# Moving the last GpSimd subtractions of the branch stage to VectorE in a three-term fp32 decoder layer

## The chip, the cores and the metric

One core of a Trainium2 chip runs the whole kernel in one launch. The metric is the device time in microseconds (us) of that core, as the median of several executions. The engines are named as in the profile: PE is TensorE (PEld its weight loads), DVE is VectorE, ACT is ScalarE, POOL is GpSimd, SP is SyncE, which here issues nearly all DMAs.

## The reference

One layer of a decoder trunk on 1024 tokens of width 1024, in float32:

```
u = rmsnorm(x) @ w_in            # 12 blocks of columns: q,k,v; retention q,k,v,g; lru x,y; 3 gates
od  = diff_attention(...)        # branch 0
o_r = silu(rg) * group_norm(retention(...))   # branch 1
o_l = rg_lru(...) * gelu(ly)     # branch 2
g   = sigmoid(gates)
merged = g0*(od @ w_branch[0]) + g1*(o_r @ w_branch[1]) + g2*(o_l @ w_branch[2])
x = x + merged @ w_out
x = x + cross_attention(rmsnorm(x), rmsnorm(mem))
x = x + relu(rmsnorm(x) @ w1)**2 @ w2
out = rmsnorm(x)
```

The part that matters here is `merged` (three products of 1024x1024 by 1024x1024, each gated and summed) and the first use of `w_out` behind it.

## The kernel before, in words

Every product is taken in a split format. A float32 matrix is held as a high part (`hi`, a rounded copy that ACT makes) and a low part (`lo`, source minus `hi`, one subtraction). The helper `split` (lines 70 and 71) issues both: the copy always on ACT, the subtraction on the engine that it is given, VectorE by default. A product is three matmuls (lines 59, 60, 61): hi by hi, hi by lo, and `lo` of the left factor by `hi`. So TensorE needs the `hi` of a left factor at line 59 and its `lo` two matmuls later, at line 61.

The branch products, the projections before them and the first MLP product run by a Strassen-Winograd scheme: a pair of weight units of 128 columns is cut into blocks A11 to A22, four sums of them are made by VectorE (`left`, line 1117), and seven block products (numbered k = 1 to 7) replace eight. For each k one left factor, here called a unit (tile `wu`, 128x512), is split by `prepare` (through `pair_unit`). The units are made ahead of the products: `h_products` writes all of them into one list (`self.line`), and each product first calls `ahead`, which emits the next one of the list. A unit takes 12 matmuls.

The pairs of the three branches are the last 12 of that list (index p from m on). For k = 1 and 2, `prepare` always puts the subtraction on VectorE. For the others it takes the engine that `prep` hands it: before, that is VectorE for k = 6 and 4 and GpSimd for k = 7, 5 and 3.

`branch` runs three times, in the order 1, 0, 2 (branch number). It runs 28 products each time. VectorE sums each finished product out of PSUM (lines 1182 to 1187 for the scheme's own sums, line 828 for the final block), multiplies by the sigmoid of the gate (line 829) and adds the accumulator of the branch before (line 831). The result goes to DRAM (line 833); in the last branch the half of the rows with n >= 4 is split straight into a resident tile (`block<-y`). Meanwhile `load_blocks` and `fill_block` load the right factors of the next branch (`block<-block`, 128x1024 subtractions on VectorE). In the last branch the left half of `w_out` is also loaded, in four pieces through one buffer `wst`, and split: VectorE takes pieces 0 and 2, GpSimd pieces 1 and 3. The other half of `w_out` is split in four further pieces by `weight` (tile `w`), whose default engine is GpSimd. Then `w_out` begins (tile `pso`).

Each engine runs its own instructions in the order in which a planner put them at compile time, by its modelled times and by program order; `after` adds that the `hi` copies of units ("wsplit") and the weight loads ("wdma") keep the order of the program. At run time nothing is reordered: an instruction that waits holds up what is behind it on its engine, and a DMA that waits on SP's queue holds up the DMAs behind it.

Of the kernel before, what the change touches and what calls it, by code (L numbers as in the profile page):

```python
# [49 lines left out]
class Kernel:  # L50
# [596 lines left out]
    def h_products(self):  # L647


        nc, v, a = self.nc, self.nc.vector, self.a  # L650
# [6 lines left out]
        cs, m = [{} for _ in jobs], len(jobs)  # L657
# [6 lines left out]
        pairs = [(c, [UNITS[kind](n, i) for i in range(2)]) for (kind, n), c in zip(jobs, cs)]  # L664
# [3 lines left out]

        def prep(p, k):
            self.pair_load(p, *pairs[p])  # L670
            self.prepare(k, pairs[p][0], v if p >= m and k in (6, 4) else nc.gpsimd)

            turns = [x for x in (0, m - 2, m + 2, m + 6, m + 10) if x <= p < x + 2]
            q, at = (p + 1, 6) if not turns else (turns[0] + 2, 3 if p > 1 else 4)
            if k == at and p == (turns or [p])[0] and q < len(pairs):
                self.pair_load(q, *pairs[q])
# [3 lines left out]
        for q in range(m, m + 12, 4):  # L680
            seq += [(q + p, k) for p in range(2) for k in self.ORDER]
            seq += [(q + p, k) for k in (self.ORDER if q < m + 8 else self.LAST) for p in (2, 3)]
        self.line = collections.deque([lambda x=x: prep(*x) for x in seq])

        def run(p, k):
# [44 lines left out]
        for p in range(2):  # L730
            run(p, 1)
            yield
# [6 lines left out]
        for k in self.H_FIRST[1:]:  # L739
            for p in range(2):  # L740
                run(p, k)
        for p in range(2, m - 2):
            for k in self.ORDER:
                run(p, k)
# [67 lines left out]
    def branch(self, order, i, right, bw, sps, nxt):  # L812

        nc, v = self.nc, self.nc.vector
        after, load = (None, None) if nxt is None else self.load_blocks(nxt)
        mT = [[None, None], [None, None]]
        cs = self.bcs[order]

        def emit(n, j, x, y):
            rows, sl = slice(n * P, (n + 1) * P), slice(j * HB, (j + 1) * HB)  # L820
            sg = bw.tile([P, HB], F32, tag="sg", name="sgb", bufs=5)
            nc.sync.dma_start(sg, self.gsp[i * D + n * P:i * D + (n + 1) * P, sl])
            nc.scalar.activation(sg, sg, AF.Sigmoid)
            if order > 0:
                pv = bw.tile([P, HB], F32, tag="pv", name="pv", bufs=3)
                nc.sync.dma_start(pv, self.acc[order - 1][rows, sl])
            o = bw.tile([P, HB], F32, tag="y", name="y", bufs=4)
            v.tensor_tensor(o, x, y, op=ALU.add)
            v.tensor_tensor(o, o, sg, op=ALU.mult)
            if order > 0:  # L830
                v.tensor_tensor(o, o, pv, op=ALU.add)
            if nxt is not None or n < 4:
                nc.sync.dma_start(self.acc[order][rows, sl], o)
            else:
                self.split(mT[j][1][:, n % 4, :], o)

        def run(p, k):
            self.ahead()
            self.product(k, cs[p], right, self.p6(sps), lambda e, j, x, y: emit(2 * p + e, j, x, y))

        for p in range(2):
            for k in self.ORDER:
                run(p, k)

                if (p, k) == (0, 1):
                    next(self.loading)
                elif (p, k) == (0, 2):
                    self.fill_block()
        if nxt is not None:
            for at, k in enumerate(self.ORDER):  # L850
                run(2, k)
                if at > 0:
                    next(load)
                run(3, k)
            self.loading = load
            return after
        w, units = [], 0
        for k in self.LAST:
            run(2, k)
            run(3, k)  # L860

            if k == 1:
                mT[0][1] = self.block(self.slotA)
            elif k == 6:
                mT[1][1] = self.block(self.slotB)
            elif k in (2, 3):
                j = 3 - k
                mT[j][0] = self.block(self.slotA)
                x = self.acc[2][:, j * HB:(j + 1) * HB].rearrange("(k p) c -> p k c", p=P)
                self.fill_block(mT[j][0], x)  # L870

            if k in (7, 5, 3, 4):
                if k in (7, 3):
                    w.append(self.block(self.slotB))
                q = units % 2
                self.split(w[-1][:, 2 * q:2 * q + 2, :], wst, (v, nc.gpsimd)[q])
                units += 1
            if k in (1, 7, 5, 3):
                wst = bw.tile([P, 2, HB], F32, tag="wst", name="wst")
                self.after("hdma", nc.sync.dma_start(wst, self.a["w_o"][0, units].rearrange("p (k c) -> p k c", k=2)))  # L880
        self.fill_block()
        return mT, w
# [468 lines left out]
    def run(self):  # L1351
        tc, nc, a = self.tc, self.nc, self.a
        pool = lambda name, bufs=1, side="right", **kw: tc.tile_pool(name=name, bufs=bufs, side=side, reuse_waits="tile", **kw)
        self.setup()
        with pool("slotA", bufs=4, side="left") as self.slotA:
            self.n_gates, self.gate_order = 0, [b * 8 + n for b in (1, 0, 2) for n in range(8)]
            with pool("ret") as self.rp, pool("rps", space=PSUM) as self.rps:
                self.retention(pool)
            with pool("att") as self.ap, pool("aps", space=PSUM) as self.aps:
                self.attention()  # L1360
            with pool("slotB", bufs=4) as self.slotB:
                with pool("sps", space=PSUM) as sps:
                    with pool("sp") as self.sp:
                        self.sps = sps
                        for _ in self.hp:
                            pass
                    with pool("bw") as bw:
                        right = self.branch(0, 1, self.right, bw, sps, 0)
                        right = self.branch(1, 0, right, bw, sps, 2)
                        mT, w0 = self.branch(2, 2, right, bw, sps, None)  # L1370
                A, B = self.slotA, self.slotB
                with pool("work") as work:
                    with pool("xps", bufs=2, space=PSUM) as xps:
                        w = [[w0[u // 2][:, u % 2 * 2:u % 2 * 2 + 2, :] for u in range(4)]]
                        w.append([self.weight(a["w_o"][1, u], 2) for u in range(4)])
                        hx = [[self.block(s) for s in (B, A)]]
                        self.w_out(0, mT, w, hx[0], work, xps)
                        hx.append([self.block(s) for s in (A, B)])
                        self.w_out(1, mT, w, hx[1], work, xps)
                        self.mem_slot()  # L1380
                        self.mem_norm(work)
                        g = self.xattn(hx, work, xps)
                    with pool("mps", space=PSUM) as self.mps:
                        self.xa_last(g)
                        self.mlp_in()
                    with pool("m2ps", bufs=6, space=PSUM) as m2ps:
                        self.mlp_out(m2ps)
# [76 lines left out]
```

## Time and profile before

| | |
|---|---|
| median of 3 runs | 2423.28 us (2419.88 to 2424.56) |
| profiled execution: its own time / its span | 2424.15 us / 2422.4 us |
| mean granted TensorE clock | 0.981 |
| PE busy over the span | 2319.7 us (96%) |
| DVE busy | 1888.0 us (78%) |
| ACT busy | 1041.4 us (43%) |
| POOL busy | 955.9 us (39%) |
| branch stage, first moved unit to the start of `w_out` | about 1243 to 1521 us |

The span goes from the first to the last instruction of the program; the execution's own time is 1.75 us longer. "Busy" adds up the time in which an engine had an instruction in work; an instruction that waits for a resource inside the engine still counts as busy. In a timeline a row gives the start (us from the span's start), the duration, the engine, the line, the tiles written and read, and in brackets the idle time before it with what ended it.

### The profile page before, as it was taken

What the parts mean: (1) busy time and instruction counts of PE and PEld (TensorE: products, weight loads), DVE (VectorE), ACT (ScalarE), POOL (GpSimd) and SP (SyncE); (2) the same over time, 40 slices, a digit from 0 to 9 for tenths busy, and PEclk for the clock granted to TensorE, in tenths of its full rate; (3) what the DMA queues carried; (4) which work ended last, traced back from release to release, by engine and by line L of the source; (5) the groups of instructions that cost most, each with busy time, mean ns of one, the idle gap of its engine ahead of it and who ended that gap; (6) DMA issues with size and microseconds to landing.
All of it is one profiled execution on the core that took longest, in us unless ns stands there. A gap on an engine that the chain in (4) does not pass through costs nothing. (4 is left out here: it accounts for less than half of the span.)

```text
span 2422.4 us, 31108 instructions
## 1 busy us (share of the span) xinstructions
PE 2319.7 (96%) x11156; PEld 1913.1 (79%) x11156; DVE 1888.0 (78%) x2909; ACT 1041.4 (43%) x1817; POOL 955.9 (39%) x621
## 2 busy tenths in 40 slices
PE   9999999999999998999999988999989999899998
PEld 7888878888887876777887767778768888788886
DVE  7677487878797788798787898344788888788896
ACT  5443355555555543554354444135442222343333
POOL 1122212222215444455431223034155555598863
PEclk9999999999999999999999999999999999999999
DMA  5222122222215354543576687343225443744341
GB/s 173 81 87 70 58 70 60 64 71 70 62 49 180 127 162 162 174 134 136 178 266 240 228 287 239 105 146 119 97 83 183 152 144 135 254 167 166 121 165 70
DMA packets 135994, 335.12 MB, mean 138 GB/s; under 512 B 17040, under 2 KB 27281, under 8 KB 135840
## 3 DMA queue, kind: packets, MB, share of 16 engines
q1 hardware_dynamic: 135264, 331.30, 41.4%
q8 instruction: 89, 1.46, 0.2%
q10 hardware_dynamic: 576, 1.84, 0.2%
q14 instruction: 65, 0.53, 0.1%
HBM read 227.64 MB, written 97.05 MB: 134 GB/s over the span
## 5 line engine op out<-in xcount | busy, mean ns | idle before, releaser
L59 PE MATMUL ps<-block,wu 128*128 128x512 f32 x1428 | 568.6, 398 | 27.2 <-DVE sf L1187 10.4
L61 PE MATMUL ps<-block,wu 128*128 128x512 f32 x1428 | 565.3, 396 | 10.2 <-DVE wu L71 10.2
L60 PE MATMUL ps<-block,wu 128*128 128x512 f32 x1428 | 561.9, 394 | 0.8 <-DVE block L71 0.8
L71 POOL TENSOR_TENSOR wu<-st,wu 128x512 fp32r<-128x512 f32 x144 | 227.3, 1585 | 303.4 <-ACT wu L70 290.4
L59 PEld LDWEIGHTS ps<-block,wu 128*128 128x128 f32 x1428 | 272.4, 191 | 89.0 <-DVE sf L1187 11.3
L61 PEld LDWEIGHTS ps<-block,wu 128*128 128x128 f32 x1428 | 271.2, 190 | 75.1 <-DVE wu L71 13.3
L60 PEld LDWEIGHTS ps<-block,wu 128*128 128x128 f32 x1428 | 271.8, 190 | 61.0 <-DVE block L71 1.3
L70 ACT CAST wu<-st 128x512 fp32r<-128x512 f32 x240 | 141.9, 620 | 210.1 <-DVE st L1117 94.1
L71 POOL TENSOR_TENSOR w<-st,w 128x1024 fp32r<-128x1024 f32 x50 | 124.6, 2501 | 176.7 <-ACT w L70 176.5
L59 PE MATMUL ps<-wu,hu 128*128 128x512 f32 x456 | 179.4, 394 | 8.0 <-ACT wu L70 4.2
L60 PE MATMUL ps<-wu,hu 128*128 128x512 f32 x456 | 178.9, 392 | 0.9 <-POOL wu L71 0.8
L61 PE MATMUL ps<-wu,hu 128*128 128x512 f32 x456 | 178.6, 392 | 0.0
L71 POOL TENSOR_TENSOR wu<-sf,wu 128x512 fp32r<-128x512 f32 x63 | 122.2, 1954 | 131.9 <-ACT wu L70 95.8
L1273 DVE TENSOR_TENSOR acc<-acc,ps 128x512 f32<-128x512 f32 x184 | 118.1, 679 | 19.8 <-PE ps L61 19.4
L71 DVE TENSOR_TENSOR hu<-sth,hu 128x1024 fp32r<-128x1024 f32 x53 | 118.1, 2231 | 14.3 <-ACT hu L70 13.6
L466 ACT ACTIVATE p<-sc,mx 128x256 f32<-128x256 f32 (+7 forms) x128 | 94.8, 742 | 69.9 <-DVE mx L463 50.1
L71 DVE TENSOR_TENSOR wu<-st,wu 128x512 fp32r<-128x512 f32 x96 | 91.1, 960 | 30.9 <-ACT wu L70 30.8
L59 PEld LDWEIGHTS ps<-wu,hu 128*128 128x128 f32 x456 | 86.3, 189 | 28.7 <-ACT wu L70 4.6
L59 PE MATMUL psk<-block,w 128*128 128x512 f32 x256 | 101.6, 397 | 0.0
L60 PEld LDWEIGHTS ps<-wu,hu 128*128 128x128 f32 x456 | 86.3, 189 | 19.3 <-POOL wu L71 1.3
L61 PE MATMUL psk<-block,w 128*128 128x512 f32 x256 | 101.2, 395 | 0.0
L60 PE MATMUL psk<-block,w 128*128 128x512 f32 x256 | 100.8, 394 | 0.0
(383 smaller groups left out, 5627.4 us busy)
## 6 DMA issues: line engine op xcount, KB each, us to landing
sth<-h SPq DMA_DIRECT2D x53, 512.0 KB, 3.2
st<-in_w SPq DMA_DIRECT2D x32, 512.0 KB, 4.2
h<-hab SPq DMA_DIRECT2D x32, 512.0 KB, 2.8
w<-in_w SPq DMA_DIRECT2D x8, 2048.0 KB
block<-oTs SPq DMA_DIRECT2D x24, 512.0 KB, 5.8
sgb<-gsp SPq DMA_DIRECT2D x48, 256.0 KB, 5.3
gsp<-l SPq DMA_DIRECT2D x44, 256.0 KB, 2.8
acc<-y SPq DMA_DIRECT2D x40, 256.0 KB, 2.9
```

Source lines behind the costliest of these rows:

```text
L59: nc.tensor.matmul(ps, lhsT=lhs.hi, rhs=rhs.hi, start=start, stop=False)
L60: nc.tensor.matmul(ps, lhsT=lhs.hi, rhs=rhs.lo, start=False, stop=False)
L61: nc.tensor.matmul(ps, lhsT=lhs.lo, rhs=rhs.hi, start=False, stop=stop)
L70: ins = self.nc.scalar.copy(dst.hi, src)
L71: self.lo_ins = (lo_engine or self.nc.vector).tensor_tensor(dst.lo, src, f32(dst.hi), op=ALU.subtract)
L466: nc.scalar.activation(p[:, 0:n], sc[:, 0:n], AF.Exp, bias=mx, accum_out=l)
L1273: v.tensor_tensor(acc[k][:, st, :], acc[k][:, st, :], ps, op=ALU.add)
```

## The change

Three lines. In the branch pairs, VectorE makes the low parts of every unit; it makes all four pieces of the first half of the output weights; and it makes the four pieces of the second half. In these 12 pairs that is 36 subtractions of 128x512 (three for each pair) and 6 of 128x1024 (two `wst` pieces and four `w` pieces). ACT's copies, the DMAs and the matmuls stay what they were.

```diff
@@ h_products, prep
-            self.prepare(k, pairs[p][0], v if p >= m and k in (6, 4) else nc.gpsimd)
+            self.prepare(k, pairs[p][0], v if p >= m else nc.gpsimd)
@@ branch
-                self.split(w[-1][:, 2 * q:2 * q + 2, :], wst, (v, nc.gpsimd)[q])
+                self.split(w[-1][:, 2 * q:2 * q + 2, :], wst)
@@ run
-                        w.append([self.weight(a["w_o"][1, u], 2) for u in range(4)])
+                        w.append([self.weight(a["w_o"][1, u], 2, lo=nc.vector) for u in range(4)])
```

## The prediction

> **What bounds the kernel now.** I began with the page's busy shares, then cut the stage that the change touches out of the span.
>
> ```profile
> span 2422.4 us, 31108 instructions
> PE 2319.7 (96%) x11156; PEld 1913.1 (79%) x11156; DVE 1888.0 (78%) x2909; ACT 1041.4 (43%) x1817; POOL 955.9 (39%) x621
> ```
>
> TensorE bounds the whole, so only time in which it idles or runs slowly can be won. The table by stretches (us, then busy us of each engine, granted clock, DMA share, GB/s), cut near the ends of the three branches and of the tail:
>
> ```profile
> 1243.00:1330.00 87.00, 86.23 (x378) 70.57 (x376) 72.58 (x90) 40.63 (x61) 18.66 (x12) 1.00 0.71 240
> 1330.00:1416.00 86.00, 80.59 (x336) 65.20 (x336) 76.61 (x99) 42.20 (x63) 20.24 (x12) 0.94 0.77 256
> 1416.00:1498.00 82.00, 74.61 (x314) 60.08 (x315) 73.57 (x97) 36.23 (x58) 28.77 (x14) 0.96 0.73 247
> 1498.00:1521.00 23.00, 11.65 (x36) 7.83 (x35) 22.97 (x23) 10.18 (x13) 10.79 (x5) 0.67 0.70 237
> ```
>
> PE is full in the first stretch, a few us short in the next two, and half idle in the last 23 us, where VectorE is busy without a break. What PE waited for in 1243 to 1521 (total, times, longest):
>
> ```profile
> PE ps L59 <- ACT wu L70: 9.8, 3, 6.7
> PE pso L59 <- ACT block L70: 9.1, 2, 5.7
> PE ps L61 <- DVE wu L71: 3.7, 3, 2.9
> PE pso L60 <- POOL block L71: 2.1, 1, 2.1
> ```
>
> That is 24.7 us, the most that could be won but for slow matmuls. Now the groups of that window on VectorE (all but small ones) and all of GpSimd (count, busy us, mean ns):
>
> ```profile
> L71 DVE TENSOR_TENSOR block<-block 128x1024 fp32r<-128x1024 f32 x38 | 51.0, 1343 | 3.8 <-ACT block L70 3.6
> L829 DVE TENSOR_TENSOR y<-y,sgb 128x512 f32<-128x512 f32 x48 | 47.7, 995 | 1.6 <-ACT sgb L823 1.3
> L71 DVE TENSOR_TENSOR wu<-st,wu 128x512 fp32r<-128x512 f32 x40 | 34.2, 860 | 7.9 <-ACT wu L70 7.9
> L828 DVE TENSOR_TENSOR y<-ps,sf 128x512 f32<-128x512 f32 x48 | 32.8, 685 | 11.3 <-DMA block<-odT 6.0 <-ACT sf L1178 5.4
> L831 DVE TENSOR_TENSOR y<-y,pv 128x512 f32<-128x512 f32 x32 | 27.5, 864 | 0.7 <-DMA pv<-acc 0.5
> L71 DVE TENSOR_TENSOR block<-y,block 128x512 fp32r<-128x512 f32 x8 | 8.2, 1030 | 2.0 <-ACT block L70 1.9
> L71 DVE TENSOR_TENSOR wu<-sf,wu 128x512 fp32r<-128x512 f32 x6 | 5.8, 969 | 3.4 <-ACT wu L70 3.4
> L71 POOL TENSOR_TENSOR wu<-sf,wu 128x512 fp32r<-128x512 f32 x18 | 33.0, 1846 | 111.6 <-ACT wu L70 75.7 <-DMA st<-in_w_br 22.4 <-DVE l L693 13.6
> L71 POOL TENSOR_TENSOR wu<-st,wu 128x512 fp32r<-128x512 f32 x18 | 30.0, 1665 | 78.9 <-ACT wu L70 78.9
> L71 POOL TENSOR_TENSOR w<-st,w 128x1024 fp32r<-128x1024 f32 x4 | 10.7, 2672 | 7.8 <-ACT w L70 7.8
> L71 POOL TENSOR_TENSOR block<-wst,block 128x1024 fp32r<-128x1024 f32 x2 | 5.3, 2640 | 12.1 <-ACT block L70 12.1
> ```
>
> GpSimd's rows are exactly the 18 + 18 + 4 + 2 = 42 moved instructions: after the change GpSimd does nothing here. And VectorE's rows of one shape differ: line 828, with one input (`ps`) from PSUM, takes 685 ns, while lines 829 and 831, with both from SBUF, average 995 and 864. A timeline around one PE wait says why (VectorE, GpSimd, PE):
>
> ```profile
> 1332.60 1.77 DVE L829 TENSOR_TENSOR y<-y,sgb 128x512 f32<-128x512 f32 x1
> 1334.30 1.75 DVE L71 TENSOR_TENSOR wu<-st,wu 128x512 fp32r<-128x512 f32 x1
> ```
> ```profile
> 1332.55 2.95 POOL L71 TENSOR_TENSOR wu<-sf,wu 128x512 fp32r<-128x512 f32 x2 [24.78 <-ACT wu L70]
> ```
> ```profile
> 1336.11 0.80 PE L61 MATMUL ps<-block,wu 128*128 128x512 f32 x1 [2.88 <-DVE wu L71]
> ```
>
> While GpSimd works, line 829 and the subtraction on VectorE take 1.77 and 1.75 us. Without it they take about 0.68: line 828 keeps that in the mean of its 48, and this piece of the tail has a quiet 128x1024, a quiet 128x512, and then one that meets GpSimd again:
>
> ```profile
> 1500.37 1.21 DVE L71 TENSOR_TENSOR block<-wst,block 128x1024 fp32r<-128x1024 f32 x1
> 1501.50 0.68 DVE L71 TENSOR_TENSOR block<-y,block 128x512 fp32r<-128x512 f32 x1
> 1502.11 2.86 DVE L829 TENSOR_TENSOR y<-y,sgb 128x512 f32<-128x512 f32 x1
> ```
>
> So a GpSimd subtraction and a VectorE instruction with both inputs in SBUF exclude each other.
>
> **The change, part by part.**
>
> Removed from VectorE: the stretching. Against 685 ns (line 828) for 512 columns and 1.21 us (1500.37) for 1024: 38 x 0.133 + 48 x 0.310 + 40 x 0.175 + 32 x 0.179 + 8 x 0.345 + 6 x 0.284 = 5.0 + 14.9 + 7.0 + 5.7 + 2.8 + 1.7 = 37.1 us, or 0.88 us for each of the 42.
>
> Added to VectorE: the 42 themselves. By the starts of the three rows above, VectorE is free again 1.13 us after one of 1024 columns and 0.61 us after one of 512 (0.60 from here on): 36 x 0.60 + 6 x 1.13 = 21.6 + 6.8 = 28.4 us. So VectorE's load falls by about 9 us of 278. That is no time by itself; it counts where PE waits.
>
> (a) The wait at 1336.11. Without GpSimd, line 829 starts at 1332.60 and frees VectorE at 1333.20, and the subtraction ends at 1333.88 instead of 1336.05: -2.2 us. Ends: 0, if moved units are put ahead of it; -2.9, all of the wait.
>
> (b) The tail, 1498 to 1521. PE (three rows), ACT (two) and GpSimd:
>
> ```profile
> 1506.87 0.80 PE L59 MATMUL pso<-block 128*128 128x512 f32 x1 [3.48 <-ACT block L70]
> 1515.89 0.80 PE L59 MATMUL pso<-block 128*128 128x512 f32 x1 [5.66 <-ACT block L70]
> 1518.83 0.80 PE L60 MATMUL pso<-block 128*128 128x512 f32 x1 [2.14 <-POOL block L71]
> ```
> ```profile
> 1514.27 0.62 ACT L70 CAST block<-y 128x512 fp32r<-128x512 f32 x1 [3.14 <-DVE y L831]
> 1514.80 1.04 ACT L70 CAST block<-wst 128x1024 fp32r<-128x1024 f32 x1
> ```
> ```profile
> 1515.92 2.86 POOL L71 TENSOR_TENSOR block<-wst,block 128x1024 fp32r<-128x1024 f32 x1 [2.23 <-ACT block L70]
> ```
>
> The last piece of `w_out` stands on ACT behind a copy that waits for VectorE's line 831, so VectorE's lateness decides, and then GpSimd's 2.86 us. What one 128x1024 of GpSimd costs VectorE lies between 0.88 scaled by duration (2.67 against 63.0 / 36 = 1.75 us: 1.3) and the 2.2 of the row at 1502.11; I take 1.6. Five of them, `wst` piece 1 and the four `w`, come before: 5 x 1.6 = 8.0 us go, 5 x 1.13 = 5.7 come, net -2.3. In the stretch 1416 to 1498 GpSimd had 14 instructions, so VectorE's load falls there by some 14 x 0.28 = 3.9 us; I take -1.0 of it as an earlier entry into the tail, since VectorE also waits there. The last piece takes 1.21 instead of 2.86 us: -1.7. Sum -5.0. Better end -9: the four `w` are not needed until `w_out` reaches its second half, and if they are put behind the rest 4.5 us more go. Worse end 0: VectorE's queue is in order, and other work may stand ahead of the last piece.
>
> (c) The moved units' own delay. On GpSimd a subtraction ran soon after its copy; on VectorE it queues. In the third branch:
>
> ```profile
> 1425.07 1.66 ACT L70 CAST wu<-st 128x512 fp32r<-128x512 f32 x3
> ```
> ```profile
> 1427.63 1.75 POOL L71 TENSOR_TENSOR wu<-st,wu 128x512 fp32r<-128x512 f32 x1
> ```
> ```profile
> 1437.43 0.68 DVE L71 TENSOR_TENSOR wu<-st,wu 128x512 fp32r<-128x512 f32 x1
> ```
> ```profile
> 1439.42 0.39 PE L61 MATMUL ps<-block,wu 128*128 128x512 f32 x1
> ```
>
> Of the three copies begun at 1425.07 the first had its low part from GpSimd at 1427.63, the second from VectorE only at 1437.43. PE used this second unit at 1439.42 (last row), 1.3 us after it was made. Units are made several products ahead and a product lasts about 2.75 us (12 matmuls; 378 in 86.23 us are 0.23 each), so the delay is mostly hidden, but here the cover is nearly gone. I take +1, ends 0 and +13 (the second rival).
>
> (d) The two other waits (9.8 us, `ps` for ACT). ACT stood there behind copies of right factors that had not landed, and their loads stand in SP's queue behind stores that wait for VectorE:
>
> ```profile
> 1420.60 1.05 ACT L70 CAST block<-block 128x1024 fp32r<-128x1024 f32 x1 [5.99 <-DMA block<-oTs]
> ```
> ```profile
> SPq L833 <- DVE y L829: 51.9, 14, 8.0
> ```
>
> SP's queue also holds weight loads until the last reader of a raw block is done, now VectorE instead of GpSimd. An earlier VectorE helps both, an added delay hurts; I take 0, ends -3 and +3.
>
> Sum: -2.2 - 5.0 + 1 + 0 = -6.2 us on the profiled execution, 2424.15 (its span of 2422.4 and 1.75 around it): 2418.0. The median shown is 0.87 lower, so 2417.1, rounded to 2417.
>
> **The rivals.**
>
> *No change: the load only changes hands.* If GpSimd's instructions cost VectorE about what they cost as its own, nothing is won where VectorE is late. Per moved unit the rows give 0.88 against 0.60, close enough that (b) shrinks to its last term and (a) to half: -1.7 - 1.1 + 1 = -1.8, so 2421.5. The Trainium skill, "Perfetto Trace Analysis", "Optimizing Scalar/DVE Operations", says that as the two engines share an SBUF read port, moving operations between them "might not help". By that rule alone the sum would be 0 and the time 2423.3; the trace agrees that they block each other, but not that the price is equal.
>
> *Slower: VectorE's queue delivers the units late.* Place: the third branch, behind ACT's long wait at 1420.60. The unit of (c) came 1.3 us ahead of its use although VectorE ran it some 11 us after its copy. A moved unit of the same bunch that is used three products (8.2 us) earlier and copied at most 2 us earlier would, with the same delay, be late by 8.2 - 2 - 1.3 = 4.9 us. After a stall PE also runs slowly: in the last stretch above 36 matmuls took 11.65 us, 0.32 each at a granted clock of 0.67, some 3.4 us too much behind two stalls or three, say 1.5 for each. Two such bunches cost 2 x (4.9 + 1.5) = 13 us in place of the +1, so -7.2 + 13 = +5.8: 2429. It decides once the stalls exceed the 7.2 us of (a) and (b). For it: GpSimd finished its unit of that bunch 4.3 us after the copy began (1427.63 + 1.75). Against it: VectorE's total falls, and the planner may place a unit early in the queue.
>
> *Better: the waits of (d) close too.* With -9 in (b) and half of 9.8: 2423.3 - 2.2 - 9 - 4.9 = 2407.
>
> **How the numbers follow.** The forecast has 0.53 (2409 to 2420), no change 0.25 (2419 to 2425), slower 0.16 (2427 to 2434), better 0.06. The range 2408 to 2427 takes in the ends of (a) and (b), all of no change and the mild edge of slower. A change of 0.2% (4.8 us) is about what a measurement tells from none: faster (under 2418.4) holds most of the forecast and all of better, 0.55; slower (over 2428.1) 0.15; the same 0.30.
>
> **What would show it.** In 1243 to 1521 GpSimd has no `wu`, `w` or `block`; lines 829 and 831 average 0.69 us; VectorE's busy time falls by some 9 us; PE's wait for the last `wst` piece starts earlier and is shorter, and GpSimd is gone from PE's waits. It is wrong if VectorE's rows stay stretched, or if "PE ps L61 <- DVE wu L71" grows beyond 3.7 us: then the order on VectorE decides.

## The result and the profile after

The changed kernel takes 2398.13 us (median of 4 runs, 2396.4 to 2400.13) against 2423.92 us for the kernel before, run beside it: a ratio of 0.9901 (95% interval 0.9883 to 0.9918). It is faster by about 25 us, four times the forecast and beyond the range. The profiled execution took 2397.62 us. The head of its page:

```profile
span 2395.8 us, 31036 instructions
PE 2309.9 (96%) x11156; PEld 1907.2 (80%) x11156; DVE 1871.9 (78%) x2951; ACT 1040.1 (43%) x1817; POOL 881.1 (37%) x579
```

The same matmuls (x11156) take 9.8 us less busy time than before, so part of the gain is not idle time but speed. The table by stretches of the changed kernel, cut as for the kernel before (us; busy us of PE, PEld, DVE, ACT, POOL; granted clock, DMA share, GB/s), and its last row beside that of the kernel before:

```profile
1243.00:1330.00 87.00, 87.00 (x382) 71.49 (x382) 74.18 (x109) 44.31 (x67) 0.00 (x0) 1.00 0.78 260
1330.00:1416.00 86.00, 81.83 (x355) 66.03 (x354) 82.20 (x122) 46.59 (x71) 0.00 (x0) 1.00 0.84 284
1416.00:1498.00 82.00, 79.73 (x345) 64.01 (x343) 78.81 (x119) 39.04 (x60) 0.00 (x0) 1.00 0.77 256
1498.00:1521.00 23.00, 20.48 (x86) 16.52 (x87) 9.32 (x13) 4.30 (x7) 1.11 (x2) 0.93 0.53 163
1243.00:1521.00 278.00, 269.03 (x1165) 218.05 (x1165) 244.50 (x361) 134.25 (x203) 1.11 (x2) 0.99 0.77 258
```
```profile
1243.00:1521.00 278.00, 253.07 (x1062) 203.68 (x1061) 245.73 (x305) 129.25 (x195) 78.45 (x42) 0.94 0.73 247
```

In the same 278 us PE gets through 1165 matmuls instead of 1062. The 103 more, at 269.03 / 1165 = 0.231 us each, are 23.8 us of work: the gain lies in this window. It has two parts. PE's idle time falls from 278 - 253.07 = 24.9 to 9.0 us, which is 16.0; and 1062 matmuls at the new pace would have taken 245.2 instead of 253.07 us, which is 7.8. What PE still waits for (total, times, longest):

```profile
PE ps L61 <- DVE wu L71: 4.2, 4, 1.4
PE pso L59 <- DVE xt L906: 2.8, 1, 2.8
PE ps L59 <- ACT wu L70: 1.5, 2, 0.8
```

The wait for ACT fell from 9.8 to 1.5 us, and both waits of `pso` for the pieces of `w_out` (9.1 and 2.1) are gone. VectorE's groups (count, busy us, mean ns), and GpSimd's only one, in the same window:

```profile
L71 DVE TENSOR_TENSOR block<-block 128x1024 fp32r<-128x1024 f32 x39 | 47.1, 1216 | 4.0 <-ACT block L70 3.8
L71 DVE TENSOR_TENSOR wu<-st,wu 128x512 fp32r<-128x512 f32 x58 | 39.1, 682 | 7.3 <-ACT wu L70 7.3
L829 DVE TENSOR_TENSOR y<-y,sgb 128x512 f32<-128x512 f32 x48 | 32.7, 682 | 1.6 <-ACT sgb L823 1.5
L828 DVE TENSOR_TENSOR y<-ps,sf 128x512 f32<-128x512 f32 x48 | 32.6, 681 | 1.0 <-PE ps L61 1.0
L831 DVE TENSOR_TENSOR y<-y,pv 128x512 f32<-128x512 f32 x32 | 21.7, 681 | 0.0
```
```profile
L97 POOL TENSOR_TENSOR rs<-rs,mhalf 128x1 f32<-128x1 f32 x2 | 1.1, 556 | 285.1 <-DVE rs L96 285.1
```

Line 829 fell from 995 to 682 ns, line 831 from 864 to 681, and nothing on VectorE in these rows is stretched any more: every 128x512 takes what line 828 takes.

To place the gain, the n-th matmul of one line and tile pair is set beside its like in another kernel (each trace has all 1428 of `ps<-block,wu` and all 64 of `pso<-block` on line 59). The columns are four such matmuls by their start in the kernel before; the entries are how much later (+) or earlier (-) they start, in us. Each row is one execution. The first column, ahead of the first stall, already spreads by up to 2 us (5.8 in one row), so differences of that size between rows mean little:

| kernel | 1294.79 (ahead of the first stall) | 1350.25 (behind it) | 1470.23 (behind the second) | 1560.16 (behind the tail) |
|---|---|---|---|---|
| after | +1.3 | -5.6 | -11.5 | -23.2 |
| units alone | -0.1 | -6.7 | -13.5 | -18.9 |
| output weights alone | -0.4 | -2.6 | -3.6 | -10.6 |
| before, GpSimd writes and reads two columns | +0.4 | -9.0 | -7.6 | -17.3 |
| after, GpSimd subtracts as well | -2.1 | -3.9 | -2.2 | +1.9 |
| before, store does not wait for lines 829 and 831 | +1.4 | -2.2 | -2.3 | -5.2 |
| after, right factors loaded by GpSimd's queue | +5.8 | +5.5 | +4.5 | -6.6 |
| after, accumulator stored by GpSimd's queue | +0.4 | -5.4 | -8.7 | -20.7 |

So three places pay: the stalls at 1329 to 1336 (6.9 us), at 1415 to 1424 (5.9 us), and the tail (11.7 us). The last 3 us of the 26.5 that the two profiled executions differ by lie behind 1560.

### The profile page after: what moved, and what is told of

Read it like the earlier page. It is cut to its first block, busy times and chain, and to the rows that moved or that the text cites. A ratio compares the mean times of both kernels' runs of the same rounds, so it can differ in the third digit from the quotient of the medians.

```text
span 2395.8 us, 31036 instructions
## 1 busy us (share of the span) xinstructions
PE 2309.9 (96%) x11156; PEld 1907.2 (80%) x11156; DVE 1871.9 (78%) x2951; ACT 1040.1 (43%) x1817; POOL 881.1 (37%) x579
## 5 line engine op out<-in xcount | busy, mean ns | idle before, releaser
L59 PE MATMUL ps<-block,wu 128*128 128x512 f32 x1428 | 565.2, 396 | 18.0 <-DVE sf L1187 9.8
L60 PE MATMUL ps<-block,wu 128*128 128x512 f32 x1428 | 559.7, 392 | 0.8 <-DVE block L71 0.8
L59 PEld LDWEIGHTS ps<-block,wu 128*128 128x128 f32 x1428 | 270.1, 189 | 79.2 <-issue 9.1
L61 PEld LDWEIGHTS ps<-block,wu 128*128 128x128 f32 x1428 | 269.9, 189 | 74.7 <-DVE wu L71 13.5
L60 PEld LDWEIGHTS ps<-block,wu 128*128 128x128 f32 x1428 | 270.0, 189 | 60.3 <-DVE block L71 1.3
L71 POOL TENSOR_TENSOR wu<-st,wu 128x512 fp32r<-128x512 f32 x126 | 202.9, 1618 | 224.3 <-ACT wu L70 211.2
L59 PE MATMUL ps<-wu,hu 128*128 128x512 f32 x456 | 178.7, 392 | 6.6 <-DVE hab L1201 4.5
L60 PE MATMUL ps<-wu,hu 128*128 128x512 f32 x456 | 178.4, 391 | 1.1 <-POOL wu L71 1.1
L71 POOL TENSOR_TENSOR w<-st,w 128x1024 fp32r<-128x1024 f32 x46 | 115.6, 2522 | 169.0 <-ACT w L70 168.9
L97 POOL TENSOR_TENSOR rs<-rs,mhalf 128x1 f32<-128x1 f32 x26 | 14.6, 562 | 414.3 <-DVE rs L96 414.3
L1273 DVE TENSOR_TENSOR acc<-acc,ps 128x512 f32<-128x512 f32 x184 | 117.9, 677 | 19.4 <-PE ps L61 18.9
L71 DVE TENSOR_TENSOR hu<-sth,hu 128x1024 fp32r<-128x1024 f32 x53 | 118.2, 2234 | 10.9 <-ACT hu L70 10.4
L71 DVE TENSOR_TENSOR wu<-st,wu 128x512 fp32r<-128x512 f32 x114 | 96.0, 852 | 29.5 <-ACT wu L70 29.5
L59 PEld LDWEIGHTS ps<-wu,hu 128*128 128x128 f32 x456 | 86.0, 189 | 27.0 <-DVE acc L1273 3.6
L59 PE MATMUL psk<-block,w 128*128 128x512 f32 x256 | 101.7, 397 | 0.0
L60 PEld LDWEIGHTS ps<-wu,hu 128*128 128x128 f32 x456 | 85.9, 188 | 19.6 <-POOL wu L71 1.4
L60 PE MATMUL psk<-block,w 128*128 128x512 f32 x256 | 100.8, 394 | 0.0
```

Of the source, the lines that this page charges most:

```text
L59: nc.tensor.matmul(ps, lhsT=lhs.hi, rhs=rhs.hi, start=start, stop=False)
L60: nc.tensor.matmul(ps, lhsT=lhs.hi, rhs=rhs.lo, start=False, stop=False)
L61: nc.tensor.matmul(ps, lhsT=lhs.lo, rhs=rhs.hi, start=False, stop=stop)
L71: self.lo_ins = (lo_engine or self.nc.vector).tensor_tensor(dst.lo, src, f32(dst.hi), op=ALU.subtract)
L97: self.nc.gpsimd.tensor_tensor(dst, dst, self.mhalf[:, : dst.shape[-1]], op=ALU.pow)
L1273: v.tensor_tensor(acc[k][:, st, :], acc[k][:, st, :], ps, op=ALU.add)
```

## The experiments

The theory at this point: GpSimd's subtractions excluded VectorE's instructions with both inputs in SBUF, VectorE was late, and its lateness went through SP's stores, the loads behind them and ACT's copies to PE. Rival: the planner's new order of the queues, and not the exclusion, made the gain.

**The parts by themselves.** In the kernel before, first line 1 of the change alone (the 36 units):

```diff
-            self.prepare(k, pairs[p][0], v if p >= m and k in (6, 4) else nc.gpsimd)
+            self.prepare(k, pairs[p][0], v if p >= m else nc.gpsimd)
```

> Only the first line of the change: the 36 units of the branches on VectorE, the output weights as before. Read from the two traces, the first matmuls of the products are 6.9 us earlier (against before) behind the wait at 1329 to 1336 and another 5.9 us behind the wait at 1415 to 1424, and the tail brings the last 13. If these parts are separate, this kernel gains the first two: 13 us, about 2411. If the tail follows from the units too (VectorE enters it earlier), it gains most of 25: 2400 to 2404. The rival of the prediction, that the two early waits are a matter of DMAs alone, expects 2 us: 2422.

Measured: 2401.81 us (2400.15 to 2403.6), ratio 0.9925 (0.9912 to 0.9939) against 2420.32 for the kernel before on that chip. Then lines 2 and 3 alone (the six pieces of the output weights):

```diff
-                self.split(w[-1][:, 2 * q:2 * q + 2, :], wst, (v, nc.gpsimd)[q])
+                self.split(w[-1][:, 2 * q:2 * q + 2, :], wst)
-                        w.append([self.weight(a["w_o"][1, u], 2) for u in range(4)])
+                        w.append([self.weight(a["w_o"][1, u], 2, lo=nc.vector) for u in range(4)])
```

> Only the other two lines: the six 128x1024 subtractions of the output weights on VectorE, the units as before. If the parts are separate, this gains the tail's 13 us: about 2411. The term of the prediction for these six (without the earlier entry) expects 4 us: 2420. If the tail's gain needs the units, it is 0 to 4 us.

Measured: 2413.10 us (2409.26 to 2415.33), ratio 0.9971 (0.9959 to 0.9983). The gains, 0.75% and 0.29%, add up to 1.04%, and the whole change gave 0.99%: within the noise the parts add up. In the table, the two stalls come from the units above all (-6.6 and -6.8, against -2.2 and -1.0 from the output weights), and the tail gets 5.4 us from the units and 7.0 from the output weights.

**The exclusion without the move.** The kernel before, but each of the 42 GpSimd subtractions is cut to two columns, and a memset by GpSimd writes the low part, which is then zero. VectorE gets no instruction that it did not have. In the traces PE's order is that of before, and so is that of the other engines but for 4 of ACT's 1824 instructions, 15 of VectorE's 2912 and 16 of SP's 824. What this kernel leaves out is these 42 low parts.

```diff
-        self.lo_ins = (lo_engine or self.nc.vector).tensor_tensor(dst.lo, src, f32(dst.hi), op=ALU.subtract)
+        self.lo_ins = sub_lo(self, dst, src, lo_engine)
...
+        self.nc.gpsimd.tensor_tensor(dst.lo[first], src[first], f32(dst.hi)[first], op=ALU.subtract)
+        for _ in range(1):
+            ins = self.nc.gpsimd.memset(f32(dst.lo), 0.0)
```

> The kernel before, but on GpSimd each of the 42 subtractions is replaced by one of two columns and a memset of the low part, so that GpSimd hardly reads SBUF there; the low parts of these 42 left factors and weights are zero. VectorE gets nothing added, and the order of the instructions on PE, ACT, VectorE and SP stays that of before but for a few dozen places. Theory 1 (the exclusion costs the time: it stretches VectorE, whose lateness holds SP's loads and ACT): lines 829 and 831 at 0.69 us, and at least the gain of the change, 2390 to 2400. Theory 2 (the planner's new order gave the time): 2420 to 2425. If GpSimd's memset excludes VectorE too, lines 829 and 831 stay above 0.8 us and nothing can be read.

Measured: 2403.26 us (2399.15 to 2405.65), ratio 0.9926 (0.9907 to 0.9944). VectorE's line 829 and GpSimd's memsets:

```profile
L829 DVE TENSOR_TENSOR y<-y,sgb 128x512 f32<-128x512 f32 x48 | 32.8, 684 | 3.6 <-ACT sgb L823 3.3
```
```profile
L1395 POOL MEMSET wu<- 128x512 f32 x36 | 19.0, 527 | 2.1
```

GpSimd still works beside VectorE (36 memsets of 527 ns, each behind a subtraction of two columns), and line 829 is not stretched. The Trainium skill, "SBUF — State Buffer", "Who interferes with whom", says that a VectorE instruction with two SBUF inputs contends with a GpSimd instruction that reads SBUF, and not with one that only writes it; 684 ns here against 995 before agree on both halves. So without the exclusion, with nothing moved and hardly anything reordered, some 17 us are won: the order of the queues is not needed for them. The relief is larger here than in the change, though, because VectorE takes nothing over: it is busy 214.2 us (third column of busy times below), against 245.7 before and 244.5 in the changed kernel. And one stall stayed, the second:

```profile
1243.00:1521.00 278.00, 264.14 (x1137) 214.28 (x1135) 214.19 (x313) 131.31 (x200) 47.91 (x85) 0.98 0.74 253
```

```profile
PE ps L59 <- ACT wu L70: 8.8, 1, 8.8
```

**The move without its relief.** The changed kernel; GpSimd makes the 42 subtractions as well, into a scratch that nobody reads. In the trace the order on PE, VectorE and SP is exactly that of the changed kernel, and on ACT one load of `x` stands at another place.

```diff
+    if eng == "twice":
...
+        for s, h in parts:
+            self.nc.gpsimd.tensor_tensor(scr, s, f32(h), op=ALU.subtract)
+        eng = None
     return (eng or self.nc.vector).tensor_tensor(dst.lo, src, f32(dst.hi), op=ALU.subtract)
```

> The changed kernel, but GpSimd makes the 42 subtractions too, into a scratch that nobody reads (as 48 of 512 columns). The order on PE, ACT, VectorE and SP is the changed kernel's, instruction for instruction; VectorE carries its 28 us more and is also excluded by GpSimd as before. Theory 1: the 25 us are lost again and more, since VectorE now has both loads: 2425 to 2450, with lines 829 and 831 stretched and the waits of PE back. Theory 2 (order): 2396 to 2402.

Measured: 2427.48 us (2422.11 to 2430.74), ratio 1.0027 (1.0016 to 1.0037): the whole gain is lost, and a little more. VectorE's groups (L1401 is the subtraction that was line 71), GpSimd's additional work (L1399), and PE's waits:

```profile
L1401 DVE TENSOR_TENSOR wu<-sf,wu 128x512 fp32r<-128x512 f32 x24 | 24.8, 1038 | 0.0
L829 DVE TENSOR_TENSOR y<-y,sgb 128x512 f32<-128x512 f32 x48 | 41.4, 863 | 0.3 <-ACT sgb L823 0.3
```
```profile
L1399 POOL TENSOR_TENSOR cm<-sf,wu 128x512 bf16<-128x512 f32 x18 | 32.2, 1786 | 115.1 <-ACT wu L70 100.4 <-DMA block<-oTs 13.8
```
```profile
PE ps L59 <- ACT wu L70: 9.7, 3, 6.3
```

The wait for ACT is back to 9.7 us (9.8 before), with GpSimd's results unread: and SP's queue waits for GpSimd nowhere in this window, so it is the stretching that brought it back. With these two runs the exclusion is shown as the main cause: lifting it in the old order wins most of the gain, and bringing it back in the new order loses all of it. They do not price the new order by itself, since VectorE here has both its own 42 subtractions and the stretching (268.2 us busy, more than in either kernel). Between the kernel with memsets (0.9926) and the changed kernel (0.9901) some 6 us are left, but their intervals overlap, and the memsets left VectorE less to do. In the table the largest difference lies at the second stall, where the one loses 1.4 us and the other gains 5.9. There the last two loads ahead of the copy are issued as follows (kernel before, then after):

```profile
1414.74 0.88 SPq L791 DMA_DIRECT2D block<-oTs  x2
```
```profile
1403.05 0.92 SPq L791 DMA_DIRECT2D block<-oTs  x2
```

With the memsets they go at 1408.06, 6.7 us earlier than before. But PE too is earlier by then: it runs out of work at 1415.47 before, at 1406.61 with the memsets and at 1409.86 in the changed kernel. Measured against PE, the loads are 2.2 us later with the memsets, and 6.1 us earlier in the changed kernel. So at this stall lifting the exclusion alone won nothing, and the changed kernel with the exclusion back lost 1.7 us there. Only the lifted exclusion and the planner's new order together closed it; which part of that order does it was not tried.

**The way from VectorE to ACT.** In the kernel before, the store of line 833 takes the gate tile `sg` instead of the product `y`, so it waits for neither line 829 nor 831; the accumulator in DRAM then holds gates.

```diff
-                nc.sync.dma_start(self.acc[order][rows, sl], o)
+                nc.sync.dma_start(self.acc[order][rows, sl], sg)
```

> The kernel before, but line 833 stores the gate tile sg (ready since ACT's sigmoid) in place of VectorE's y, so that SP's queue does not wait for VectorE at these 40 stores; what is accumulated is then wrong. All subtractions stay on GpSimd, so the exclusion stays. The planner's order shifts in some places. If SP's queue is the way by which VectorE's lateness reaches the loads of right factors and ACT, PE's waits for ACT in the branches (9.8 us before, at 1329 and 1415) fall under 4 us and the time by 5 to 10: 2410 to 2417. If these loads are late because the DMA engines are busy (share 0.7 to 0.9 there), the waits stay and the time is 2418 to 2424.

Measured: 2415.27 us (2411.87 to 2419.13), ratio 0.9984 (0.9973 to 0.9995). PE's waits:

```profile
PE ps L61 <- DVE wu L71: 8.6, 4, 2.9
PE pso L59 <- ACT block L70: 7.4, 2, 6.5
PE ps L59 <- ACT wu L70: 2.3, 1, 2.3
```

The wait for ACT falls from 9.8 to 2.3. That fits the path: VectorE late, store waiting in SP's queue, loads behind it late, ACT's copy late. It does not prove it, because the planner also ordered otherwise (114 of VectorE's 2912 and 126 of SP's 824 instructions stand elsewhere). Nor is the queue free: the stores now wait for the gates,

```profile
SPq L833 <- ACT sgb L823: 59.4, 26, 7.2
```

where before they waited 51.9 and 48.7 us for VectorE's lines 829 and 831, and the loads of gates and of the accumulator (lines 822 and 826) still wait for VectorE. PE's own wait for VectorE grows from 3.7 to 8.6, the second stall is as long as before in the table, and only 0.16% is won: who takes one wait out of this chain meets the late engine one step on.

**The same queue in the changed kernel.** First the loads of right factors moved from SP's queue to GpSimd's (with a key of their own for the order), then the stores of line 833 instead.

```diff
-                self.after("hdma", self.nc.sync.dma_start(f32(b.lo[:, 2 * q:2 * q + 2, :]), x[:, 2 * q:2 * q + 2, :]))
+                self.after("bdma", self.nc.gpsimd.dma_start(f32(b.lo[:, 2 * q:2 * q + 2, :]), x[:, 2 * q:2 * q + 2, :]))
```

> The changed kernel with the loads of right factors (fill_block) issued on GpSimd's queue, which is idle there. They no longer stand behind stores that wait for VectorE. PE's waits in the branches are only some 6 us in the changed kernel, of which 1.5 are for ACT: 2394 to 2399 if the queue on SP is what held them; 2400 or more if the issue on GpSimd costs more than the place in SP's queue.

```diff
-                nc.sync.dma_start(self.acc[order][rows, sl], o)
+                nc.gpsimd.dma_start(self.acc[order][rows, sl], o)
```

> The changed kernel with the stores of line 833 issued on GpSimd's queue, so that no load on SP waits for VectorE there. By the theory of the queue ACT waits less for sgb and block loads (39.5 and 27.5 us in the changed kernel), PE gains what is left of its waits, up to 4 us: 2393 to 2398. If the waits of ACT are covered already: no difference, 2396 to 2400.

Measured: 2417.06 us (2411.96 to 2421.85), ratio 0.9989 (0.9975 to 1.0004), for the loads, and 2401.11 us (2399.86 to 2405.22), ratio 0.9932 (0.9917 to 0.9947), for the stores, against 2420.04 for the kernel before. Neither is better than the change itself. With the loads moved, ACT waits longer for the gates, whose loads stayed on SP (39.5 us in the changed kernel), and PE has one long wait for ACT:

```profile
ACT sgb L823 <- DMA sgb<-gsp: 70.6, 25, 6.7
```
```profile
1429.39 0.80 PE L59 MATMUL ps<-block,wu 128*128 128x512 f32 x1 [8.37 <-ACT wu L70]
```

How much of this loss is the other queue and how much the planner's new order was not separated.

**How far the exchange pays.** In the changed kernel VectorE makes the low parts of all other units of that list as well, those of the projections ahead of the branches.

```diff
-            self.prepare(k, pairs[p][0], v if p >= m else nc.gpsimd)
+            self.prepare(k, pairs[p][0], v)
```

> The changed kernel with the other 125 units of GpSimd in the stage before (the projections, 722 to 1243 us) on VectorE as well. If the price per unit is as in the branches (0.88 released, 0.60 added), VectorE's load falls there by some 30 us of 429 and PE's 29 us of waits shrink: 2380 to 2392. If VectorE there is so full that units come late (it has scans and convolutions of several us in its queue, and GpSimd keeps other work, so that part of the exclusion stays): 2400 to 2420.

Measured: 2372.67 us (2369.05 to 2374.89), ratio 0.981 (0.9794 to 0.9826), by the ratios some 22 us better than the change (the profile shows 115 units moved, not 125). The stretch of the projections, in the changed kernel and in this one:

```profile
722.00:1243.00 521.00, 492.08 (x2116) 396.78 (x2115) 429.11 (x471) 249.43 (x358) 243.44 (x145) 0.98 0.48 162
```
```profile
722.00:1243.00 521.00, 504.11 (x2195) 408.30 (x2194) 445.71 (x608) 270.56 (x382) 39.84 (x30) 0.99 0.52 174
```

GpSimd falls from 243 to 40 us, VectorE makes 137 more instructions in 17 us more, and PE 79 more matmuls. Two waits for VectorE's own work (`psr L60 <- DVE xcs L71` 12.6 and `ps L59 <- DVE sf L1187` 9.8) are 0.7 and gone, while the wait for units grows from 3.3 to 13.8: the next limit. From this kernel three steps further, into the MLP: the units of its first product (98), the weights of its second product (49), and both with the 28 sums of raw weights (line 1117).

```diff
-            c["u", k] = self.pair_unit(c["w"][self.LEFT[k]], self.nc.vector if p < 2 else self.nc.gpsimd)
+            c["u", k] = self.pair_unit(c["w"][self.LEFT[k]], self.nc.vector)
```

> This is the kernel in which VectorE makes all low parts of units in the projections and the branches (2372.67 us), and now also those of the first MLP product: 98 subtractions of 128x512 leave GpSimd. Theory that TensorE's waits decide: VectorE's load falls by some 98 x 0.28 = 27 us, but in the stretch 1755 to 2065 TensorE is busy 300.4 of 310 us, and its waits there for VectorE are 8.5 us (ps L59 <- DVE hab L1201 4.4, ut L1184 4.1). So at most 9.6 us can go; I expect 0 to 7, take 3: 2369 to 2370. Rival, a gain in proportion to the moved subtractions (25 us for 115 in the stages before, 0.22 each): 98 x 0.22 = 21 us, 2351. Rival, units late in VectorE's queue: ps L61 <- DVE wu L71 grows above 10 us in the MLP, 2378 or more.

```diff
-            w, h = self.w2_unit(raw[self.LEFT[k]], g), self.h1_unit(c, self.RIGHT[k])
+            w, h = self.w2_unit(raw[self.LEFT[k]], v), self.h1_unit(c, self.RIGHT[k])
```

> The kernel in which VectorE makes all low parts of units in the projections and the branches (2372.67 us), and now also those of the weights of the second MLP product but the last four: 49 or so subtractions of 128x1024 leave GpSimd, whose sums of raw weights (line 1117, 28 of 128x1024) stay. Theory that TensorE's waits decide: TensorE is busy 295.7 of 305 us there and waits for VectorE 3.0 us (acc L1273) and 2.5 us (wu L71): gain 0 to 5, take 2: 2371; hu <- sth,hu falls from 2.18 us towards 1.5. Rival, proportion to the moved elements (0.22 us for each 512 columns): 49 x 2 x 0.22 = 22 us, 2351. Rival, VectorE full: it is busy 255 of 305 us, and 49 x 1.13 = 55 us come in while fewer than that go, so it becomes the bound, 2380 or more.

```diff
-        self.left(raw, *(self.xw.tile([P, 2, HB], F32, tag=t, name="s2", bufs=2) for t in ("xt", "xt", "ts")), self.nc.gpsimd)
+        self.left(raw, *(self.xw.tile([P, 2, HB], F32, tag=t, name="s2", bufs=2) for t in ("xt", "xt", "ts")), self.nc.vector)
```

> Both MLP edits together, and the 28 sums of raw weights of the second MLP product (line 1117) moved to VectorE too: GpSimd has almost nothing left behind the branches but the four first parts of the cross attention's weights and small rows. Theory that TensorE's waits decide: at most the 9.6 + 9.3 us that TensorE idles in the two MLP stretches; VectorE's load in the second: 255 busy - 53 x 0.97 (hu from 2.18 to 1.21 us) - about 6 + (49 + 28) x 1.13 = 285 of 305 us, 93%, so the sums are near the edge: I expect 2365 to 2378, take 2371. Rival, proportion: 2330. Rival, VectorE full: 2385 or more, with ps L59 <- DVE wu or acc L1273 waits above 15 us in the second MLP product.

Measured, against 2420.11 for the kernel before: 2373.84 us (2369.93 to 2380.47), ratio 0.9813 (0.9797 to 0.9829), for the first product; 2366.2 us (2364.65 to 2369.54), ratio 0.9777 (0.9764 to 0.9791), for the second; 2372.99 us (2370.21 to 2378.34), ratio 0.9809 (0.9796 to 0.9823), for both with the sums. The stretch of the first MLP product, without and with its 98 units moved:

```profile
1755.00:2065.00 310.00, 300.39 (x1291) 244.70 (x1290) 256.11 (x295) 78.42 (x130) 179.36 (x110) 0.98 0.47 165
```
```profile
1755.00:2065.00 310.00, 300.42 (x1288) 244.86 (x1288) 259.78 (x394) 77.57 (x129) 28.87 (x13) 0.98 0.48 160
```

GpSimd loses 150 us and VectorE takes 99 more instructions in 4 us more, a better exchange than in the branches; yet PE does the same number of matmuls, since it hardly waited there. That decides between a gain in proportion to what is moved (2351 was expected by it) and one that only PE's waits allow. The second product gave 6.5 us (2372.67 to 2366.2), a little above the 0 to 5 that its waits allowed. This kernel, 2.2% faster than the kernel before, is the fastest of all that ran. The one with both edits and the sums is not better; why it lost about as much again stays open.

## Why the prediction was wrong

The direction was right, and so was the exclusion as its cause; the size was not. What failed is the path from VectorE to PE: step (d), put at nothing, and the slow matmuls behind the stalls, left out of the sum; step (b) was sized too small. The steps, with what the profile after shows for each (from the lists of PE's waits and the two totals above):

| step | forecast us | measured us | how |
|---|---|---|---|
| (a) wait at 1336.11 | -2.2 | -2.2 | the same matmul waits 0.71 instead of 2.88 |
| (c) late units | +1 | +2.7 | waits for `wu`: 4.2 - 0.7 = 3.5, before 3.7 - 2.9 = 0.8 |
| (d) waits of `ps` for ACT | 0 | -8.3 | 9.8 to 1.5 |
| (b) tail | -5.0 | -8.4 | 9.1 + 2.1 to nothing, 2.8 new |
| slow matmuls behind stalls | not in the sum | -7.8 | 253.07 - 245.2 |
| sum | -6.2 | -24.0 | 103 matmuls more: 23.8 |

- **The load of VectorE was right.** The forecast was some 9 us less. Unstretched, its rows are 681 to 688 ns and 1.22 us, as taken; from 1243 to the start of the second half of `w_out` (1524.77 before, 1500.09 after) its busy time is 246.5 and 237.3 us, so -9.2.
- **(a) and (c) were right in kind, and (a) to the tenth by luck.** It was worked out for VectorE's old order, with line 829 ahead of the subtraction; in the changed kernel the planner put line 829 earlier, the subtraction ends at 1331.6 instead of the 1333.88 of the forecast, and PE comes earlier too. This is the row of step (a), and one of the new waits of (c):

```profile
1331.65 0.50 PE L61 MATMUL ps<-block,wu 128*128 128x512 f32 x1 [0.71 <-DVE wu L71]
1341.55 0.50 PE L61 MATMUL ps<-block,wu 128*128 128x512 f32 x1 [1.38 <-DVE wu L71]
```

- **The sign of being wrong.** The prediction named it: PE's wait for VectorE's units beyond 3.7 us. It is 4.2 us, so the sign came, but the time fell all the same; this wait is small beside those that went.
- **(d) is the step that failed first.** The prediction had the chain (VectorE, store, load, copy, PE) and the rows, and took 0 between -3 and +3, a bound from no row. ACT's copy at the second stall still waits 5.62 us for its load, but it comes 11.6 us earlier and PE has only 0.77 us left to wait:

```profile
1409.01 1.05 ACT L70 CAST block<-block 128x1024 fp32r<-128x1024 f32 x1 [5.62 <-DMA block<-oTs]
```
```profile
1410.63 0.50 PE L59 MATMUL ps<-block,wu 128*128 128x512 f32 x1 [0.77 <-ACT wu L70]
```

Where each step of a chain waits for VectorE, the relief can add up along it: by then the stage's VectorE rows had been stretched by some 19 us (9.9 and 9.5 in its first two stretches, summed over the rows above their quiet duration). This is not the whole of it: the run with memsets, which lifts the exclusion and keeps the order, still has 8.8 us of this wait, and the run that brings the exclusion back into the new order has 9.7. In these two runs neither took it away by itself. The rival "better" had half of these waits, at 0.06.
- **(b): the better end came true.** The four `w` were put behind the last piece, as that end had it, and the copy of the last piece no longer stands behind one that waits for VectorE's line 831. VectorE (the last piece; three of the `w`, the fourth at 1501.88) and PE:

```profile
1491.34 1.22 DVE L71 TENSOR_TENSOR block<-wst,block 128x1024 fp32r<-128x1024 f32 x1
...
1495.95 3.48 DVE L71 TENSOR_TENSOR w<-st,w 128x1024 fp32r<-128x1024 f32 x3
```
```profile
1493.29 0.39 PE L60 MATMUL pso<-block 128*128 128x512 f32 x1
```

The matmul that waited 2.14 us at 1518.83 follows without a wait. The term "-1.0 as an earlier entry" was the small one: the units alone gave 5.4 us in the tail.
- **Slow matmuls were priced on one side only.** The rival "slower" charged 1.5 us for the slow matmuls behind each new stall; the forecast credited nothing for those behind the stalls that it removed, and these were 7.8 us.
- **"No change" and the skill's "might not help".** The Trainium skill, "Perfetto Trace Analysis", "Optimizing Scalar/DVE Operations", makes the exchange of work between the two engines doubtful because they share a port. The two engines do exclude each other here, but that speaks for the move: over the 42 moved instructions, one on GpSimd held VectorE for 0.88 us on average and costs it 28.4 / 42 = 0.68 as its own (the 0.60 that the prediction set beside the 0.88 is for 512 columns alone).
- **"Slower" did not come.** The longest wait for a unit is 1.4 us, against the 4.9 that this rival feared.

## What to carry to other kernels

Where two engines exclude each other, compare for each instruction what it holds the busier one up with what it costs there as its own, and move it only in stages where the engine that sets the time waits; 98 units moved where PE hardly waited gave nothing. Follow the lateness of a busy engine through queues that are in order, and give the chain a price from its own rows, not nothing. Here the order of the queues had its part in that price, so a range with a source would have had to reach from none of these waits to all of them. A stall that goes takes the slow matmuls behind it along where it had halved the clock, so credit these too.

## What the hardware showed beside this

Whether a stall halves TensorE's clock does not go by its length alone. In these traces the granted clock changes only at steps of 3.41 us, and what counts is how much of such a window PE idles. The kernel before, around the first stall, window by window (us; PE busy and matmuls; granted clock, DMA share, GB/s):

```profile
1325.09:1328.50 3.41, 3.41 (x17) 1.00 0.86 206
1328.50:1331.92 3.42, 0.73 (x4) 1.00 1.00 392
1331.92:1335.33 3.41, 1.22 (x2) 0.50 0.97 380
1335.33:1338.74 3.41, 2.63 (x6) 0.50 0.77 250
1338.74:1342.16 3.42, 3.42 (x9) 0.50 0.59 155
1342.16:1345.57 3.41, 3.41 (x16) 1.00 0.88 307
```

PE idled 2.78 us from 1329.23 and then 2.88 us from 1333.22. The first window with idle time, 2.69 us of it, is followed by half the clock; the clock came back behind a window that PE filled. From 1336.11 to 1341.82 the matmuls came every 0.43 us instead of every 0.23: some 2.8 us lost beside the waits themselves. Two other stalls of the same trace, one of 2.52 us at 1784.79 and one of 1.68 us at 756.10:

```profile
1782.48:1785.89 3.41, 2.31 (x11) 1.00 0.31 123
1785.89:1789.30 3.41, 2.00 (x9) 1.00 0.02 5
1789.30:1792.72 3.42, 3.42 (x17) 1.00 0.00 0
```
```profile
755.07:758.48 3.41, 1.54 (x6) 1.00 1.01 389
758.48:761.89 3.41, 2.85 (x7) 0.50 1.02 418
```

The longer one lies across the edge of two windows (1.10 and 1.41 us idle) and costs no clock; the shorter one lies in one window, which idles 1.87 us in all, and halves it. Over the 13 traces of this case, no window at full clock with less than 1.59 us of idle time was followed by half the clock, and every one with more than 1.92 us was. The Trainium skill, "TensorE: Matmul & The Clock Gate", "Part 1: The HAM clock gate (the "warmup" mystery)", gives an idle window of about 3.4 us for the fall to half speed and about as much busy time for the way back. The length of the window and the way back agree with these rows; the fall needs less than a whole idle window here, about half of one.
